# A hybrid encoder layer: the u tiles read from a transposed copy, the low parts of the v tiles on another engine

## The chip, the cores and the metric

The kernel runs on one core of one Trainium2 chip. The metric is the device time of one execution in microseconds, median of three runs. The engines are called as in the profile: PE (TensorE, with PEld for its weight loads), DVE (VectorE), ACT (ScalarE), POOL (GpSimd) and SP, which issues the plain transfers.

## What is computed

One layer of an encoder: projections, attention, two recurrent scans, and at its end a retrieval feed-forward over 16384 experts of one neuron each, which is the part that the change touches. For 1024 tokens of width 1024, eight heads choose 16 experts each, so 128 per token.

```python
def peer_ffn(h, w_query, sub_keys1, sub_keys2, expert_u, expert_v):
    ...
    v1, i1 = lax.top_k(s1, PEER_TOPK)
    v2, i2 = lax.top_k(s2, PEER_TOPK)
    cand = (v1[..., :, None] + v2[..., None, :]).reshape(T, PEER_HEADS, PEER_TOPK * PEER_TOPK)
    top_s, top_p = lax.top_k(cand, PEER_TOPK)
    ...
    def block(args):
        xc, ic, gc = args
        u = jnp.take(expert_u, ic, axis=0)
        act = jax.nn.gelu(jnp.einsum('cd,ced->ce', xc, u).astype(jnp.float32), approximate=False)
        vv = jnp.take(expert_v, ic, axis=0)
        return jnp.einsum('ce,ced->cd', (gc * act).astype(vv.dtype), vv)
```

## The kernel before

The first 1200 us are the rest of the layer. The retrieval then treats its eight blocks of 128 tokens in two ways.

**Three blocks gather.** For each of 128 choices, `fetch` (L1364) brings the rows of u that the 128 tokens want into a tile gu (128x1024), and later the rows of v into gv: one indirect transfer each, issued by POOL. DVE multiplies gu by the tokens and sums (L1392), and adds gv times its weight to gacc (L1400). `gathers` is called from all later stages to spread these 384 pairs; each fetch is tied to the latest POOL product by `pace`, so that it comes behind it in POOL's queue, and is written two choices ahead of its use (`LAG`). Four buffers each hold gu and gv in the last stage.

**Five blocks go dense.** All 16384 experts are computed for 640 tokens, in 128 tiles of 128 experts, with weights that are zero for experts that were not chosen. A tile n needs:

- `u_load` (L1439): the 128x1024 tile of u, one expert per partition, two buffers.
- `u_transpose`: PE transposes it in eight blocks of 128x128 into two put banks (L1449); from each bank ACT rounds the high part uTh (L1452), DVE subtracts to get the low part uTl (L1458).
- `act_half`, twice: 24 products of 128x320 in three terms (high by high, low by high, high by low, L317 to L319) into a bank pact, and the GELU on ACT (L1467). put and pact share a ring of three banks.
- `gate`: the activations times the dense weights, on POOL (L1794), split into ah on ACT (L1795) and al on DVE (L1796).
- `v_load` and `v_split`: half a v tile, 128x512, as vr (four buffers), vh on ACT (L1814), and vl = vr - vh on POOL (L1815). vh and vl have three buffers each.
- `v_steps`: five token blocks by three products (L1835 to L1837) into five banks py; after four tiles DVE adds the five banks into yac (L1844).

The first 65 tiles (`early`) are brought up to the GELU in the stages before and stored; the last stage reads them back (gl). 21 of them run beside the queries, 24 beside the choice of experts, 20 beside the making of the dense weights, where POOL, DVE and ACT make one-hot tiles `o` (L1720). In the last stage the tiles go in groups of four: while PE does the eight v steps of one group (two halves of four tiles), the gates of the next are made, and the two tiles of it that are not early go through u products, one after each half.

The order on each engine comes from the scheduler of the framework, from the order in which the calls are written and from the dependences; each engine then works through its queue in order. `split` forms are in float32 rounded for the PE (`FR`).

Of the kernel before, what the change touches and what calls it, by code (L numbers as in the profile page):

```python
# [8 lines left out]
F32 = mybir.dt.float32  # L9
FR = mybir.dt.float32r  # L10
# [3 lines left out]
AF = mybir.ActivationFunctionType  # L14
ALU = mybir.AluOpType
# [5 lines left out]
D = 1024  # L21
NB = 8
NK = 8
# [40 lines left out]
NGL = 2  # L64
NACC = 2
NWH = 2
ULP = (-1, 1)
NUR = 1
NS_ = 3
TC = 32  # L70
NSTB = 2
# [10 lines left out]
def body(tc, nc, I, out, dbg=None):  # L82
# [3 lines left out]
    with root:  # L86
# [21 lines left out]
        ident = ct([128, 128], "ident")  # L108
# [54 lines left out]
        def acp(o_, i_):  # L163
            nc.scalar.activation(o_, i_, AF.Copy)  # L164
# [56 lines left out]
        for k in range(NK):  # L221
            for i in range(2):
                a = slot("adw")
# [58 lines left out]
        def mod_steps():  # L282
# [22 lines left out]

            L = []
            for m in range(4):
                L += [lambda m=m, k=k: one(m, k) for k in range(NK)]
                L.append(lambda m=m: fin(m))
            return L  # L310

# [1018 lines left out]
        HT = TD // 2  # L1330
        NT = 128
        U, V = I["peer_u"][0], I["peer_v"][0]
        Ue = U.rearrange("(a b) d -> b a d", b=128)
        Ve = V.rearrange("(a b) d -> b a d", b=128)
        TW = "tile"
        pe = ES()
# [2 lines left out]
        lpa = pe.enter_context(tc.tile_pool(name="lpa", bufs=2, reuse_waits=TW))  # L1339
        pas = ES()  # L1340
        pa = [pas.enter_context(tc.tile_pool(name="pa", bufs=3, space=PSUM, reuse_waits=TW))]
# [80 lines left out]
        pace = [None]  # L1422
# [5 lines left out]
                next(gt, None)  # L1428


        uts, ats, urp = {}, {}, []
        early = [n for n in range(NT) if (n + 1) * NEARLY // NT > n * NEARLY // NT]
        seq = early + [n for n in range(NT) if n not in early]
        after = dict(zip(seq, seq[1:]))
        actd = dram.tile([NEARLY, 128, TD], F32, name="actd")

        def u_load(n):
            u = lpa.tile([128, D], F32, name="u", bufs=NU)
            nc.sync.dma_start(u, Ue[n])  # L1439
            uts[n] = [u]  # L1440

        def u_transpose(n, kh):
            if kh == 0:
                uts[n] += [lpa.tile([128, NK, 128], FR, name="uTh"), lpa.tile([128, NK, 128], FR, name="uTl")]
            u, uh, ul = uts[n]
            pt = pa[0].tile([128, 512], F32, name="put", tag="a")
            for i in range(4):
                k = kh * 4 + i
                nc.tensor.transpose(pt[:, i * 128:(i + 1) * 128], u[:, k * 128:(k + 1) * 128], ident)  # L1449
            ks = slice(kh * 4, kh * 4 + 4)  # L1450
            p3 = pt.rearrange("p (k e) -> p k e", k=4)
            nc.scalar.activation(uh[:, ks], p3, AF.Copy)  # L1452
            if n in early and early.index(n) <= ULP[0] and kh >= ULP[1]:
                ur = urp[0].tile([128, 512], F32, name="ur", bufs=NUR)
                acp(ur, pt)
                nc.gpsimd.tensor_tensor(ul[:, ks], ur.rearrange("p (k e) -> p k e", k=4), uh[:, ks], ALU.subtract)
            else:
                nc.vector.tensor_tensor(ul[:, ks], p3, uh[:, ks], ALU.subtract)  # L1458

        def act_half(n, hf):  # L1460
            _, uh, ul = uts[n]
            if hf == 0:
                ats[n] = lpa.tile([128, TD], F32, name="gl", bufs=NGL)
            sl = slice(hf * HT, hf * HT + HT)
            ps = pa[0].tile([128, 512], F32, name="pact", tag="a")
            mm3(ps[:, 0:HT], [(uh[:, k, :], ul[:, k, :], dTh[:, k, sl], dTl[:, k, sl]) for k in range(NK)])
            nc.scalar.activation(ats[n][:, sl], ps[:, 0:HT], AF.Gelu)  # L1467
            if hf == 1 and n in early:
                nc.sync.dma_start(actd[early.index(n)], ats[n])

        def tile_steps(n):
            L = [lambda: act_half(n, 0), lambda: act_half(n, 1)]
            if n in after:
                m = after[n]
                L = [lambda: u_transpose(m, 0), L[0], lambda: u_transpose(m, 1), L[1]]
                if m in after:
                    L[0] = lambda: (u_load(after[m]), u_transpose(m, 0))
            return L


        with ES() as qs:
            q1 = qs.enter_context(tc.tile_pool(name="q1", bufs=1, reuse_waits=TW))
            q2 = qs.enter_context(tc.tile_pool(name="q2", bufs=2, reuse_waits=TW))
            urp.append(q2)
            pq = qs.enter_context(tc.tile_pool(name="pq", bufs=5, space=PSUM, reuse_waits=TW))

            def qbank(name):
# [20 lines left out]
            pt = qbank("pt")  # L1508
# [156 lines left out]
            for L in hl[:NGB]:  # L1665
                for f in L:
                    f()
            u_transpose(seq[0], 0)
            u_transpose(seq[0], 1)
            merge((Q1, 0, 1), (sum(hl[NGB:], []), 0.1, HE))  # L1670
            cg, cd = [c_steps(tb) for tb in range(NGB)], [c_steps(tb) for tb in range(NGB, NB)]
            tl_ = [tile_steps(n) for n in early]
# [126 lines left out]
        vts = {}  # L1799
# [10 lines left out]
        def v_split(i):  # L1810
            if i < len(vseq) and not isinstance(vts[i], tuple):
                vh = lp.tile([128, 512], FR, name="vh", bufs=NV)
                vl = lp.tile([128, 512], FR, name="vl", bufs=NV)
                nc.scalar.activation(vh, vts[i], AF.Copy)  # L1814
                pace[0] = nc.gpsimd.tensor_tensor(vl, vts[i], vh, ALU.subtract)  # L1815
                vts[i] = vh, vl

        def v_steps(g):
# [49 lines left out]
        for g in range(NT // GR + 1):  # L1868
# [3 lines left out]
            if g < NT // GR:  # L1872
                at(s0, g_load, g)
                for k, n in enumerate(order[g]):
# [3 lines left out]
                    else:  # L1878
                        L = tile_steps(n)
                        if TRY and n in after:  # L1880
                            L = [L[1], lambda L=L, k=k: (L[3](), [at(now[0] + TRY[i], L[2 * i]) for i in range(2)])]
# [37 lines left out]
```

## Time and profile before

| | |
|---|---|
| three runs | 4042.25, 4057.20, 4059.28 us (median 4057.2) |
| the profiled execution | 4056.53 us, its span 4054.8 us |
| PE busy over the span | 3468.1 us (86%), granted clock 0.928 |
| DVE | 3047.6 us (75%) |
| POOL | 2316.8 us (57%) |
| ACT | 1261.6 us (31%) |
| transposes of u | 1024 on PE, 1215.6 to 3981.3 us |
| vl on POOL | 256, 2404.1 to 4038.4 us |

Busy time counts an engine's instructions; the products of PE are pipelined and overlap each other. The granted clock is a share of the full TensorE clock. A wait is put down to the engine that released it last. "issue" as a releaser is time for which the profile names no other engine.

### The profile page before, as it was taken

The page shows a single profiled execution, that of the slowest core. Times are in us where ns is not written, and L with a number is a line of the kernel's source. Part 1 is how long each engine was busy: PE and PEld are TensorE (multiplying, and loading weights), DVE is VectorE, ACT ScalarE, POOL GpSimd, SP SyncE. Part 2 cuts the span into 40 slices and gives each one's busy share as a digit, 9 for nine tenths or more (in the row PEclk, how much of TensorE's full clock was granted, in tenths as well). Part 3 has the DMA queues.
Part 4 walks back from the last instruction along what each step waited for, and adds up shares of the span by engine and source line. Part 5 has one row for each costly group of instructions (what it writes and reads, how often), then busy time and mean ns, then how long its engine had stood idle before and what let it go on. Part 6 is the DMA issues. An engine that isn't in the chain of part 4 may idle for free. (4 is left out here: it accounts for less than half of the span.)

```text
span 4054.8 us, 62013 instructions
## 1 busy us (share of the span) xinstructions
PE 3468.1 (86%) x22961; PEld 3038.1 (75%) x22961; DVE 3047.6 (75%) x6082; ACT 1261.6 (31%) x2528; POOL 2316.8 (57%) x1762
## 2 busy tenths in 40 slices
PE   5978899988787878988888878889888988889898
PEld 4757877776787877878877766777777877777787
DVE  6776556776567999799788877777677878877765
ACT  3244344444213222222555532221222222222221
POOL 2132112221434466366699978777777877878774
PEclk9978998888898989999999989999899999999999
DMA  6543444343445366466798998777788888777774
GB/s 191 178 144 103 141 116 98 97 111 104 136 164 184 104 219 238 141 218 214 239 296 278 301 309 277 264 259 269 255 273 285 281 272 275 272 265 271 256 258 154
DMA packets 493462, 862.81 MB, mean 213 GB/s; under 512 B 149348, under 2 KB 290404, under 8 KB 489064
## 3 DMA queue, kind: packets, MB, share of 16 engines
q1 hardware_dynamic: 372840, 447.20, 34.3%
q0 software_dynamic: 113280, 411.63, 29.7%
q8 instruction: 181, 2.97, 0.3%
q10 hardware_dynamic: 7040, 0.03, 0.1%
q14 instruction: 121, 0.99, 0.1%
HBM read 741.91 MB, written 116.80 MB: 212 GB/s over the span
## 5 line engine op out<-in xcount | busy, mean ns | idle before, releaser
L1392 DVE SCALAR_TENSOR_TENSOR gu<-gu,ghr 128x1024 f32<-128x1024 f32 x384 | 590.3, 1538 | 301.5 <-DMA gu<-in_peer_u_dram,ei 296.2
L317 PE MATMUL pact<-dTh,uTh 128*128 128x320 f32 x2048 | 663.6, 324 | 72.2 <-DVE uTl L1458 68.3
L1400 DVE SCALAR_TENSOR_TENSOR gacc<-gv,gact,gacc 128x1024 f32<-128x1024 f32 x381 | 614.0, 1611 | 117.1 <-DMA gv<-in_peer_v_dram,ei 116.1
L319 PE MATMUL pact<-dTh,uTl 128*128 128x320 f32 x2048 | 651.3, 318 | 19.2 <-DVE uTl L1458 19.2
L318 PE MATMUL pact<-dTl,uTh 128*128 128x320 f32 x2048 | 650.3, 318 | 0.0
L1835 PE MATMUL py<-vh,ah 128*128 128x512 f32 x1280 | 531.7, 419 | 137.5 <-DVE yac L1844 77.4
L1364 POOL DMA_INDIRECT gu<-in_peer_u_dram,ei x384 | 517.9, 1349 | 86.2 <-issue 44.2
L1836 PE MATMUL py<-vl,ah 128*128 128x512 f32 x1280 | 529.1, 413 | 38.2 <-POOL vl L1815 38.2
L1364 POOL DMA_INDIRECT gv<-in_peer_v_dram,ei x384 | 477.9, 1245 | 115.0 <-issue 101.5
L1837 PE MATMUL py<-vh,al 128*128 128x512 f32 x1280 | 523.7, 409 | 4.5 <-DVE al L1796 4.5
L317 PEld LDWEIGHTS pact<-dTh,uTh 128*128 128x128 f32 x2048 | 400.8, 196 | 89.4 <-DVE uTl L1458 78.5
L1815 POOL TENSOR_TENSOR vl<-vr,vh 128x512 fp32r<-128x512 f32 x256 | 367.2, 1435 | 146.1 <-issue 116.5
L1835 PEld LDWEIGHTS py<-vh,ah 128*128 128x128 f32 x1280 | 254.9, 199 | 218.0 <-ACT vh L1814 68.8
L319 PEld LDWEIGHTS pact<-dTh,uTl 128*128 128x128 f32 x2048 | 400.1, 195 | 21.4 <-DVE uTl L1458 21.3
L318 PEld LDWEIGHTS pact<-dTl,uTh 128*128 128x128 f32 x2048 | 400.6, 196 | 2.6
L1836 PEld LDWEIGHTS py<-vl,ah 128*128 128x128 f32 x1280 | 255.2, 199 | 99.6 <-POOL vl L1815 51.4
L1467 ACT ACTIVATE gl<-pact 128x320 f32<-128x320 f32 x256 | 111.2, 437 | 632.8 <-PE pact L319 601.1
L1837 PEld LDWEIGHTS py<-vh,al 128*128 128x128 f32 x1280 | 255.2, 199 | 62.0 <-DVE al L1796 6.8
L1795 ACT ACTIVATE ah<-gl 128x640 fp32r<-128x640 f32 x128 | 92.7, 737 | 653.6 <-POOL gl L1794 552.0
L1720 POOL TENSOR_SCALAR o<-io,tT 128x128 f32<-128x128 f32 x160 | 232.5, 1457 | 35.7 <-ACT tT L164 27.5
L1741 PE MATMUL pgb<-o,o 128*128 128x128 f32 x1280 | 184.0, 290 | 64.8 <-POOL o L1720 56.4
L1814 ACT ACTIVATE vh<-vr 128x512 fp32r<-128x512 f32 x256 | 157.0, 624 | 226.3 <-PE py L1837 181.8
(1445 smaller groups left out, 7527.1 us busy)
## 6 DMA issues: line engine op xcount, KB each, us to landing
u<-in_peer_u_dram SPq DMA_DIRECT2D x128, 512.0 KB, 5.8
vr<-in_peer_v_dram SPq DMA_DIRECT2D x256, 256.0 KB, 4.0
Gd<-st SPq DMA_DIRECT2D x160, 256.0 KB, 7.1
actd<-gl SPq DMA_DIRECT2D x65, 320.0 KB, 4.4
gl<-actd SPq DMA_DIRECT2D x65, 320.0 KB, 4.8
awt<-in_ada_w_dram SPq DMA_DIRECT2D x32, 512.0 KB, 6.4
wraw<-in_peer_w_query_dram SPq DMA_DIRECT2D x32, 512.0 KB, 4.0
wraw<-in_w_in_dram SPq DMA_DIRECT2D x26, 512.0 KB, 5.1
```

Of the source, the lines that this page charges most:

```text
L317: nc.tensor.matmul(ps, lh, rh, start=(i == 0), stop=False)
L318: nc.tensor.matmul(ps, lh, rl, start=False, stop=False)
L319: nc.tensor.matmul(ps, ll, rh, start=False, stop=(i == n - 1))
L1364: g_ = nc.gpsimd.indirect_dma_start(out=r_, out_offset=None, in_=src, in_offset=bass.IndirectOffsetOnAxis(ap=eid[tb][:, j:j + 1], axis=0))
L1392: nc.vector.scalar_tensor_tensor(u, u, 1.0, hr, op0=ALU.mult, op1=ALU.mult, accum_out=act[:, q:q + 1])
L1400: nc.vector.scalar_tensor_tensor(acc, v, pact[:, q:q + 1], acc, op0=ALU.mult, op1=ALU.add)
L1720: r_ = eng.tensor_scalar(o1[:, q], io128, tT[:, 0, t:t + 1], tT[:, 2, t:t + 1], op0=ALU.is_equal, op1=ALU.mult)
L1741: nc.tensor.matmul(pg[:, q * 128:(q + 1) * 128], o1[:, 4 * x_ + q], o2[:, 4 * x_ + q], start=True, stop=True)
L1815: pace[0] = nc.gpsimd.tensor_tensor(vl, vts[i], vh, ALU.subtract)
L1835: nc.tensor.matmul(ys[hf][b], ah[:, ts], vh, start=(n == tiles[0]), stop=False)
L1836: nc.tensor.matmul(ys[hf][b], ah[:, ts], vl, start=False, stop=False)
L1837: nc.tensor.matmul(ys[hf][b], al[:, ts], vh, start=False, stop=(n == tiles[-1]))
```

## The change

The host writes a second copy of u beside the first, in which tile n already lies with the model dimension on the partitions. `u_load` reads that copy, `u_split` replaces `u_transpose`: one ACT copy and one DVE subtraction of 128x1024, both from SBUF, and no work on PE. The gathers go on reading the first copy. In `v_split` the subtraction goes to DVE, and `pace` is then set by the gate alone. The step that was the second pair of transposes is left empty, so that the number of steps stays.

```diff
-        Ue = U.rearrange("(a b) d -> b a d", b=128)
+        Ut = I["peer_ut"]
...
         def u_load(n):
+            if n in uts:
+                return
             u = lpa.tile([128, D], F32, name="u", bufs=NU)
-            nc.sync.dma_start(u, Ue[n])
+            nc.sync.dma_start(u, Ut[n])
             uts[n] = [u]
...
-        def u_transpose(n, kh):
...
-            for i in range(4):
-                k = kh * 4 + i
-                nc.tensor.transpose(pt[:, i * 128:(i + 1) * 128], u[:, k * 128:(k + 1) * 128], ident)
...
-            nc.scalar.activation(uh[:, ks], p3, AF.Copy)
...
-                nc.vector.tensor_tensor(ul[:, ks], p3, uh[:, ks], ALU.subtract)
+        def u_split(n):
+            u_load(n)
+            if len(uts[n]) > 1:
+                return
+            u = uts[n][0]
+            uh, ul = lpa.tile([128, NK, 128], FR, name="uTh"), lpa.tile([128, NK, 128], FR, name="uTl")
+            u3 = u.rearrange("p (k e) -> p k e", k=NK)
+            nc.scalar.activation(uh, u3, AF.Copy)
+            nc.vector.tensor_tensor(ul, u3, uh, ALU.subtract)
+            uts[n] += [uh, ul]
...
-                L = [lambda: u_transpose(m, 0), L[0], lambda: u_transpose(m, 1), L[1]]
+                L = [lambda: u_split(m), L[0], lambda: None, L[1]]
...
-                pace[0] = nc.gpsimd.tensor_tensor(vl, vts[i], vh, ALU.subtract)
+                nc.vector.tensor_tensor(vl, vts[i], vh, ALU.subtract)
...
+    a = inputs["peer_u"]
+    a = _np.ascontiguousarray(_np.asarray(a)[0].reshape(128, 128, NK, 128).transpose(1, 3, 2, 0)).reshape(128, 128, D)
+    arrays["in_peer_ut_dram"] = a
```

POOL's queue in the last stage, before: gl is the gate product, vl the low part, gu and gv the gathers.

```order
L1794 TENSOR_TENSOR gl_34594<-gl_34594,gt__34536 128x640
L1815 TENSOR_TENSOR vl_34694<-vr_34538,vh_34693 128x512
L1364 DMA gu_34712<-in_peer_u_dram,ei2_11948 128x1024
L1364 DMA gv_34714<-in_peer_v_dram,ei2_11948 128x1024
L1815 TENSOR_TENSOR vl_34744<-vr_34567,vh_34743 128x512
L1364 DMA gu_34762<-in_peer_u_dram,ei2_11948 128x1024
L1364 DMA gv_34764<-in_peer_v_dram,ei2_11948 128x1024
```

The same queue now:

```order
L1786 TENSOR_TENSOR gl_32587<-gl_32587,gt__32300 128x640
L1362 DMA gu_32706<-in_peer_u_dram,ei2_11948 128x1024
L1362 DMA gv_32708<-in_peer_v_dram,ei2_11948 128x1024
L1362 DMA gu_32735<-in_peer_u_dram,ei2_11948 128x1024
L1362 DMA gv_32737<-in_peer_v_dram,ei2_11948 128x1024
L1362 DMA gu_32769<-in_peer_u_dram,ei2_11948 128x1024
L1362 DMA gv_32771<-in_peer_v_dram,ei2_11948 128x1024
```

Between two pairs of gathers there stood a vl; now up to four pairs follow each other, with only gl between.

DVE's queue in the last stage, before, from the last of the five additions on:

```order
L1844 TENSOR_TENSOR yac4_23250<-yac4_23250,py_33665 128x512
L1400 SCALAR_TENSOR_TENSOR gacc_29896<-gv_33897,gact_32957,gacc_29896 128x1024
L1392 SCALAR_TENSOR_TENSOR gu_33945,gact_33745<-gu_33945,ghr_29100 128x1024
L1400 SCALAR_TENSOR_TENSOR gacc_29896<-gv_33947,gact_32957,gacc_29896 128x1024
L1392 SCALAR_TENSOR_TENSOR gu_33977,gact_33745<-gu_33977,ghr_29100 128x1024
L1400 SCALAR_TENSOR_TENSOR gacc_29896<-gv_33979,gact_32957,gacc_29896 128x1024
L1796 TENSOR_TENSOR al_33952<-gl_33816,ah_33951 128x640
L1458 TENSOR_TENSOR uTl_33909<-put_33910,uTh_33908 128x512
L1458 TENSOR_TENSOR uTl_33909<-put_33917,uTh_33908 128x512
```

And now, from behind the last of the five additions:

```order
L1807 TENSOR_TENSOR vl_32110<-vr_31945,vh_32109 128x512
L1390 SCALAR_TENSOR_TENSOR gu_32000,gact_31589<-gu_32000,ghr_27960 128x1024
L1788 TENSOR_TENSOR al_32097<-gl_31972,ah_32096 128x640
L1398 SCALAR_TENSOR_TENSOR gacc_28708<-gv_32002,gact_30854,gacc_28708 128x1024
L1807 TENSOR_TENSOR vl_32142<-vr_31974,vh_32141 128x512
L1390 SCALAR_TENSOR_TENSOR gu_32090,gact_31589<-gu_32090,ghr_27960 128x1024
L1398 SCALAR_TENSOR_TENSOR gacc_28708<-gv_32092,gact_30854,gacc_28708 128x1024
L1390 SCALAR_TENSOR_TENSOR gu_32128,gact_31589<-gu_32128,ghr_27960 128x1024
L1398 SCALAR_TENSOR_TENSOR gacc_28708<-gv_32130,gact_30854,gacc_28708 128x1024
L1450 TENSOR_TENSOR uTl_32292<-u_32101,uTh_32291 128x1024
L1788 TENSOR_TENSOR al_32135<-gl_32011,ah_32134 128x640
L1807 TENSOR_TENSOR vl_32169<-vr_32069,vh_32168 128x512
```

The low parts of v stand between the gathered operations, with one or two pairs of them between two vl, and uTl is one operation from u and uTh.

## Rows read from the trace of the kernel before

**Rows 1.** First line of the page.

```profile
span 4054.8 us, 62013 instructions
```

**Rows 2.** Busy time by stretch: length, PE, PEld, DVE, ACT, POOL, clock, DMA, GB/s.

```profile
1360.00:1680.00 320.00, 269.26 (x1762) 264.29 (x1760) 291.04 (x998) 85.30 (x162) 163.40 (x108) 0.91 0.53 180
1680.00:1925.00 245.00, 203.65 (x1316) 196.62 (x1316) 243.54 (x612) 56.27 (x104) 154.76 (x103) 0.94 0.64 217
1925.00:2370.00 445.00, 373.97 (x2599) 353.12 (x2598) 363.28 (x654) 250.34 (x594) 380.92 (x278) 0.95 0.86 279
2390.00:4055.00 1665.00, 1462.95 (x7280) 1246.11 (x7279) 1243.00 (x1361) 353.81 (x656) 1266.63 (x894) 0.95 0.77 263
```

**Rows 3.** Groups, 2390 to 4055: busy us, mean ns | idle before, releasers.

```profile
L1835 PE MATMUL py<-vh,ah 128*128 128x512 f32 x1280 | 531.7, 419 | 137.5 <-DVE yac L1844 77.4 <-ACT vh L1814 59.6
L1836 PE MATMUL py<-vl,ah 128*128 128x512 f32 x1280 | 529.1, 413 | 38.2 <-POOL vl L1815 38.2
...
L1400 DVE SCALAR_TENSOR_TENSOR gacc<-gv,gact,gacc 128x1024 f32<-128x1024 f32 x262 | 437.6, 1670 | 99.9 <-DMA gv<-in_peer_v_dram,ei 99.1
L1392 DVE SCALAR_TENSOR_TENSOR gu<-gu,ghr 128x1024 f32<-128x1024 f32 x248 | 409.8, 1653 | 273.3 <-DMA gu<-in_peer_u_dram,ei 273.1
L1815 POOL TENSOR_TENSOR vl<-vr,vh 128x512 fp32r<-128x512 f32 x256 | 367.2, 1435 | 146.1 <-issue 116.5 <-ACT vh L1814 24.7 <-DVE yac L1844 2.1
L1364 POOL DMA_INDIRECT gu<-in_peer_u_dram,ei x247 | 338.3, 1370 | 40.3 <-issue 27.3 <-ACT vh L1814 1.1 <-DVE uTl L1458 0.8
L1364 POOL DMA_INDIRECT gv<-in_peer_v_dram,ei x264 | 334.5, 1267 | 78.0 <-issue 72.0 <-DVE gu L1392 3.7 <-DVE yac L1844 1.7
...
L1844 DVE TENSOR_TENSOR yac<-yac,py 128x512 f32<-128x512 f32 x310 | 195.3, 677 | 17.0 <-PE py L1837 17.0
...
L1796 DVE TENSOR_TENSOR al<-gl,ah 128x640 fp32r<-128x640 f32 x127 | 129.1, 1033 | 25.0 <-ACT ah L1795 24.9
...
L1458 DVE TENSOR_TENSOR uTl<-put,uTh 128x512 fp32r<-128x512 f32 x122 | 78.1, 678 | 0.9 <-ACT uTh L1452 0.5
```

**Rows 4.** Waits, 2390 to 4020: us in total, times, longest us.

```profile
ACT ah L1795 <- POOL gl L1794: 542.7, 92, 14.2
```

**Rows 5.** Timeline, 3105 to 3116: start us, us, engine, line [idle before].

```profile
3105.83 0.61 ACT L1814 ACTIVATE vh<-vr 128x512 fp32r<-128x512 f32 x1
...
3106.58 1.53 POOL L1815 TENSOR_TENSOR vl<-vr,vh 128x512 fp32r<-128x512 f32 x1 [1.42 <-issue]
3108.26 1.39 POOL L1364 DMA_INDIRECT gu<-in_peer_u_dram,ei  x1
...
3115.69 2.83 DVE L1392 SCALAR_TENSOR_TENSOR gu<-gu,ghr 128x1024 f32<-128x1024 f32 x1 [4.51 <-DMA gu<-in_peer_u_dram,ei]
```

**Rows 6.** Timeline of PE, 2545 to 2547: eight transposes and the next product.

```profile
2545.36 1.04 PE L1449 MATMUL put<-ident,u 128*128 128x128 f32 x8
2546.15 0.48 PE L1835 MATMUL py<-vh,ah 128*128 128x512 f32 x1
```

**Rows 7.** Single lines, whole span: duration ns min/median/max, first and last start.

```profile
L1392 DVE SCALAR_TENSOR_TENSOR gu<-gu,ghr x384: 1195/1221/7777, 1403.3 to 3909.9; 128x1024 f32<-128x1024 f32 x192
L1400 DVE SCALAR_TENSOR_TENSOR gacc<-gv,gact,gacc x381: 1220/1284/4451, 1472.5 to 3997.2; 128x1024 f32<-128x1024 f32 x191
L1796 DVE TENSOR_TENSOR al<-gl,ah x128: 807/815/2648, 2389.1 to 4020.4; 128x640 fp32r<-128x640 f32 x128
L1415 DVE TENSOR_TENSOR gacc<-gacc,gr x3: 1209/1216/2551, 2444.4 to 4000.8; 128x1024 f32<-128x1024 f32 x3
L1857 DVE TENSOR_TENSOR yac<-yac,gr x10: 684/688/691, 4029.7 to 4050.0; 128x512 f32<-128x512 f32 x10
```

**Rows 8.** Busy time of L1794 (gl on POOL) in the last stage.

```profile
2390.00:4055.00 1665.00, 228.54 (x127) 0.95 0.77 263
```

**Rows 9.** Groups, of 1680 to 1925 and of 1925 to 2370.

```profile
L1400 DVE SCALAR_TENSOR_TENSOR gacc<-gv,gact,gacc 128x1024 f32<-128x1024 f32 x31 | 56.0, 1806 | 0.0
...
L1720 POOL TENSOR_SCALAR o<-io,tT 128x128 f32<-128x128 f32 x160 | 232.5, 1457 | 35.7 <-ACT tT L164 27.5 <-issue 6.2
```

More of the change, by code (lines that the diff above doesn't have):

```diff
@@ L66 @@
 NWH = 2
-ULP = (-1, 1)
-NUR = 1
 NS_ = 3
@@ L1428, in gathers @@
                 next(gt, None)
-        uts, ats, urp = {}, {}, []
+        uts, ats = {}, {}
         early = [n for n in range(NT) if (n + 1) * NEARLY // NT > n * NEARLY // NT]
@@ L1437, in u_load @@
         def u_load(n):
+            if n in uts:
+                return
             u = lpa.tile([128, D], F32, name="u", bufs=NU)
-            nc.sync.dma_start(u, Ue[n])
+            nc.sync.dma_start(u, Ut[n])
             uts[n] = [u]
-        def u_transpose(n, kh):
[L1443 to L1446, printed above, removed]
-            for i in range(4):
-                k = kh * 4 + i
-                nc.tensor.transpose(pt[:, i * 128:(i + 1) * 128], u[:, k * 128:(k + 1) * 128], ident)
-            ks = slice(kh * 4, kh * 4 + 4)
-            p3 = pt.rearrange("p (k e) -> p k e", k=4)
-            nc.scalar.activation(uh[:, ks], p3, AF.Copy)
[L1453 to L1457, printed above, removed]
-                nc.vector.tensor_tensor(ul[:, ks], p3, uh[:, ks], ALU.subtract)
+        def u_split(n):
[8 more added lines that the diff above has]
+            uts[n] += [uh, ul]
         def act_half(n, hf):
+            u_split(n)
             _, uh, ul = uts[n]
@@ L1474, in tile_steps @@
                 m = after[n]
-                L = [lambda: u_transpose(m, 0), L[0], lambda: u_transpose(m, 1), L[1]]
+                L = [lambda: u_split(m), L[0], lambda: None, L[1]]
                 if m in after:
-                    L[0] = lambda: (u_load(after[m]), u_transpose(m, 0))
+                    L[0] = lambda: (u_load(after[m]), u_split(m))
             return L
@@ L1483, in body @@
             q2 = qs.enter_context(tc.tile_pool(name="q2", bufs=2, reuse_waits=TW))
-            urp.append(q2)
             pq = qs.enter_context(tc.tile_pool(name="pq", bufs=5, space=PSUM, reuse_waits=TW))
@@ L1667, in body @@
                     f()
-            u_transpose(seq[0], 0)
-            u_transpose(seq[0], 1)
+            u_split(seq[0])
             merge((Q1, 0, 1), (sum(hl[NGB:], []), 0.1, HE))
@@ L1913 @@
         args[name] = nc.dram_tensor(f"in_{name}_dram", a.shape, mybir.dt.from_np(a.dtype), kind="ExternalInput").ap()
+    a = inputs["peer_u"]
+    a = _np.ascontiguousarray(_np.asarray(a)[0].reshape(128, 128, NK, 128).transpose(1, 3, 2, 0)).reshape(128, 128, D)
+    arrays["in_peer_ut_dram"] = a
+    args["peer_ut"] = nc.dram_tensor("in_peer_ut_dram", a.shape, mybir.dt.from_np(a.dtype), kind="ExternalInput").ap()
     o = nc.dram_tensor("out_0_dram", (1, T, D), F32, kind="ExternalOutput").ap()
```

## Prediction

> **What bounds the kernel now.** I read first the table by stage, then the groups of the last stage with the idle time before them, then the waits, then two short pieces of the timeline. The span is 4054.8 us [rows 1]; the profiled execution took 4056.53 us, so 1.7 us lie around the span, and it stands 0.7 us under the median of 4057.2 us. I make the sum against 4056.5.
>
> Four stretches contain nearly everything that the change touches [rows 2]. From 1360 to 1680 us queries and 21 early u tiles share the core; DVE is busy 291 of 320 us, PE 269. From 1680 to 1925 DVE is busy 243.5 of 245 us: it is the bound. From 1925 to 2370 POOL is busiest, 381 of 445 us. The dense stage from 2390 to the end, 1665 us, is where both edits meet: PE is busy 1463 us at a granted clock of 0.95, DVE 1243, POOL 1267, the DMA engines 77%. No engine is full there; the stage is three in-order queues waiting for each other.
>
> The waits say how. PE is idle 202 us (1665 - 1463): 77.4 for the additions that empty the py banks (DVE) and 59.6 for vh (ACT), both ahead of L1835, and 38.2 for vl (POOL) ahead of L1836 [rows 3]. ACT itself sits 542.7 us behind ah, waiting for the gate product on POOL [rows 4], and vh is queued behind ah. DVE is idle 422 us, of which 372 are waits for gathered rows: 273 ahead of gu, 99 ahead of gacc [rows 3]. A piece of timeline shows why they come late: POOL waits 1.42 us for a vl to start, which it does 0.14 us after ACT has ended its vh (3105.83 + 0.61), works on it 1.53 us, only then issues a gather at 3108.26, and DVE stands 4.51 us until a gather has landed, at 3115.69 [rows 5]. POOL is thus the engine that feeds DVE, and the 256 vl (367.2 us of work and 146.1 us of waiting before them, [rows 3]) sit in the middle of its queue.
>
> **The change part by part.** *Transposes out.* A tile had 8 transposes. Eight in a row start at 2545.36 and the next product starts at 2546.15 [rows 6]: 0.79 us of PE per tile. The dense stage has 122 halves uTl, so 61 tiles [rows 3]: 61 x 0.79 = 48 us less PE work, 1463 - 48 = 1415. In the three stretches before, 21 + 24 + 20 = 65 tiles give 51 us at most, but there PE waits for others.
>
> *u split from SBUF.* Two DVE operations of 0.678 us per tile become one of 128x1024. The nearest row is a plain SBUF operation of that size, 1.21 us at the least [rows 7], so 61 x 1.21 = 74 against 78.1 us [rows 3]: no gain to speak of. ACT's copy changes in the same way, and ACT is busy 354 of 1665 us [rows 2], which hides it.
>
> *vl from POOL to DVE.* POOL loses 367 of its 1267 us. DVE gets 256 operations of 128x512; the row with two SBUF inputs of that shape is 0.688 us [rows 7], so +176 us. DVE's sum becomes 1243 - 78 + 74 + 176 = 1415 us, the same as PE's. But DVE operations with two SBUF inputs are now stretched when POOL works beside them: gacc has mean 1.670 against a median of 1.284, gu 1.653 against 1.221, al 1.033 against 0.815 [rows 3, 7], together 262 x 0.386 + 248 x 0.432 + 127 x 0.218 = 236 us, while yac, which has one input in PSUM, keeps 0.677 [rows 3]. POOL's products in the stage are vl 367 and gl 228.5 us [rows 3, 8]; vl is 62% of them, so 146 us of the stretch should go with it. DVE then lies between 1415 (no relief) and 1269 us (relief by share); I take the middle, about 1340.
>
> The rule behind the stretch is in the Trainium skill, SBUF — State Buffer, section Who interferes with whom: a VectorE instruction with two SBUF inputs and a GpSimd instruction that reads SBUF exclude each other for the whole instruction. It speaks against the first edit: uTl had one input in PSUM and will have two in SBUF, as vl has on its new engine. If each of the 61 uTl waited for a whole gl of 1.80 us [rows 8], that would be 110 us more on DVE; by the shares above it is some 25.
>
> *Where the waits go.* On POOL the gathers no longer stand behind vl, which waits for vh, which waits for a vh buffer that PE must free. They stand behind gl and behind the release of one of four row buffers of each kind, which DVE gives back. So gathers should be issued further ahead and the 372 us shrink. The new wait: vl is now in DVE's queue behind gathered operations, with PE behind it. The order on DVE has one or two gather pairs between two vl; a pair is 1.28 + 1.22 = 2.5 us [rows 7], so up to 5 us for a step of PE that takes 15 products. Three vh buffers let DVE run ahead by two steps. For PE I leave the vl wait at its present 38 us, with DVE for POOL; I take away half of the vh wait (30 us), since ACT gets gl earlier, and some 40% of the py wait (32 us), since DVE idles less before the additions. With the transposes: -48 - 30 - 32 = -110 us for the dense stage. The ends are -48 - 202 (every PE wait gone) and, above nothing, the third rival below.
>
> *Earlier stages.* From 1680 DVE decides: 24 tiles, each 2 x 0.678 - 1.21 = 0.15 us less, against a stretch such as gacc shows there (1.806 against 1.284, [rows 9]), 0.52 us, if uTl gets it too: +9 us at most. From 1925 POOL decides, with 160 one-hot operations of 1.457 us [rows 9]; 20 tiles of transposes off PE do nothing for it, and if each uTl held POOL for its whole 1.21 us it would be +24 us. From 1360, 21 x 0.79 = 17 us less PE work, where PE is idle 51 of 320 us. Between -51 and +33 I take -12 us, since only the first of the three has PE near its end.
>
> Sum: 4056.5 - 110 - 12 = 3934.5, so **3934 us**, 3.0% less.
>
> **The rivals.** *First, the queues come apart more than that.* If the gathers are far enough ahead that DVE hardly waits, PE is left with its 1415 us and some 60 us of waits: 1475 for the dense stage, -190, and -25 before it: about 3840 us. For it: DVE at 1269 to 1340 us leaves room, and the DMA engines, 0.77 x 1665 = 1282 us, too. Against: three sums within 10% of each other rarely run without waits, and in each half DVE must add five banks before PE can go on.
>
> *Second, DVE takes the place of POOL and little is won.* No relief, since the remaining 127 gl find DVE with two SBUF inputs nearly always: 1415 us, half the gather waits (186) and the other 50 of its idle time: 1651 us, -14, and nothing before it: about 4040 us. The rule cited above is this one's reason. For it: DVE's sum has grown to that of PE. Against: gl alone would have to cause the stretch that vl and gl cause now.
>
> *Third, slower.* DVE serves its queue in order, so a vl behind a gather that has not landed stops PE. If the gather waits stay at 372 us although POOL is free, because landing and not issue sets them, DVE needs 1269 + 372 + 50 = 1691 us, +26: about 4083 us; without relief 1837, +172: 4228 us. It decides from the point where the remaining gather waits exceed 346 us (with relief) or 200 us (without). For it: a wait as long as 4.51 us [rows 5] is more than the vl buffers cover in one step. Against: the same gathers' wait began with POOL's late issue.
>
> That the change does not do what it says can be left out: in the new order PE has no transpose of u, and POOL no vl.
>
> **How the numbers follow.** Forecast 0.50 (own range 3885 to 3990), first rival 0.20 (3800 to 3885), second 0.18 (3990 to 4077), third 0.12. The range leaves out the outer part of the first rival and most of the third: 3835 to 4060. A difference under 0.5%, 20 us, can hardly be told from none here, since the runs before lie 17 us apart. Faster by more: 0.50 + 0.20 + 0.10 of the second = 0.80; within: the other 0.08; slower: 0.12.
>
> **What would show it.** Right, step by step: POOL's busy time in the dense stage falls by about 367 us; waits of gu and gacc for their DMA fall below 200 us; gacc and gu have means near 1.4 us; vl on DVE takes 0.69 us; PE waits less for yac and vh, and its wait for vl names DVE. The stretch from 1680 to 2370 keeps its length. Wrong: gu waits as long as before with POOL idle (third rival), gacc still at 1.65 us (second), or PE idle over 202 us with DVE vl as its releaser.

## The result and the profile after

The changed kernel takes **3919.6 us** (median, 3914.6 to 3922.8) against 4057.9 us of the kernel before on the same chip: a ratio of 0.9667 with a 95% interval of 0.9645 to 0.9690. The forecast was 3934 us. The profiled execution took 3917.25 us, its span is 3915.5 us, 139 us less than before. In the text a stage begins with its first product: the dense stage with the first py, the weights stretch before it with the first pgb. The busy times of after by these marks (length, PE, PEld, DVE, ACT, POOL, granted clock, DMA, GB/s):

```profile
1303.60:1923.70 620.10, 518.77 (x3298) 507.99 (x3297) 601.01 (x1888) 161.66 (x286) 354.44 (x224) 0.92 0.59 196
1923.70:2370.40 446.70, 340.52 (x2255) 320.90 (x2254) 354.63 (x607) 238.25 (x549) 398.76 (x279) 0.90 0.87 280
2370.40:3915.50 1545.10, 1387.90 (x6792) 1190.03 (x6792) 1204.51 (x1556) 353.90 (x594) 844.96 (x638) 0.95 0.77 283
```

By the same marks the three stretches of before are 646.4, 434.8 and 1665.2 us long. The dense stage gives 120 us, the queries and the choice of experts 26, the 1304 us ahead of them 5 (less than the 17 us by which single executions of the kernel before differ), and the weights stretch takes 12 back. In the dense stage [rows 2] POOL's busy time falls from 1267 to 845 us, DVE's from 1243 to 1205, PE's from 1463 to 1388. PE's idle time falls from 202 to 157 us.

The groups of the dense stage of after, 2370 to the end, answer to [rows 3] (busy us, mean ns | idle before, releasers):

```profile
L1828 PE MATMUL py<-vl,ah 128*128 128x512 f32 x1280 | 527.6, 412 | 64.1 <-DVE vl L1807 63.5
L1827 PE MATMUL py<-vh,ah 128*128 128x512 f32 x1280 | 523.7, 410 | 93.1 <-DVE yac L1836 64.3 <-ACT vh L1806 13.9 <-ACT uTh L1449 9.3
...
L1398 DVE SCALAR_TENSOR_TENSOR gacc<-gv,gact,gacc 128x1024 f32<-128x1024 f32 x262 | 360.0, 1374 | 55.5 <-DMA gv<-in_peer_v_dram,ei 50.6 <-issue 4.6
L1390 DVE SCALAR_TENSOR_TENSOR gu<-gu,ghr 128x1024 f32<-128x1024 f32 x248 | 320.2, 1292 | 138.2 <-DMA gu<-in_peer_u_dram,ei 131.8 <-issue 6.4
...
L1836 DVE TENSOR_TENSOR yac<-yac,py 128x512 f32<-128x512 f32 x310 | 190.5, 675 | 0.9 <-PE py L1829 0.8
...
L1807 DVE TENSOR_TENSOR vl<-vr,vh 128x512 fp32r<-128x512 f32 x256 | 181.5, 713 | 12.6 <-ACT vh L1806 12.6
L1788 DVE TENSOR_TENSOR al<-gl,ah 128x640 fp32r<-128x640 f32 x128 | 103.7, 830 | 130.3 <-ACT ah L1787 130.3
L1450 DVE TENSOR_TENSOR uTl<-u,uTh 128x1024 fp32r<-128x1024 f32 x60 | 83.5, 1392 | 5.9 <-ACT uTh L1449 5.9
```

DVE's waits for gathered rows have gone from 372 to 182 us (131.8 + 50.6). The stretch of its operations with two SBUF inputs is mostly gone: gacc from 1.670 to 1.374 us, gu from 1.653 to 1.292, al from 1.033 to 0.830, while yac keeps its 0.675. PE waits less for yac and vh, and more for vl, which is DVE's now. The waits behind the gate answer to [rows 4] (us in total, times, longest):

```profile
ACT ah L1787 <- POOL gl L1786: 287.9, 62, 7.8
POOL gl L1786 <- DMA gl<-actd: 252.6, 22, 17.8
DVE al L1788 <- ACT ah L1787: 130.3, 32, 10.9
```

ACT's wait for the gate product has halved. Another stands behind it: POOL waits 253 us, up to 17.8 us at a time, for the early tiles' activations to be loaded into a gl buffer. A piece of the timeline shows what hangs on one such wait (start us, us, engine, line [idle before]):

```profile
3017.74 1.56 POOL L1786 TENSOR_TENSOR gl<-gl,gt__27670 128x640 f32<-128x640 f32 x1 [16.15 <-DMA gl<-actd]
3019.26 1.57 POOL L1786 TENSOR_TENSOR gl<-gl,gt__27290 128x640 f32<-128x640 f32 x1
3020.98 0.98 POOL L1362 DMA_INDIRECT gu<-in_peer_u_dram,ei  x1
...
3029.88 0.94 POOL L1362 DMA_INDIRECT gv<-in_peer_v_dram,ei  x1 [0.30 <-issue]
...
3020.86 1.37 ACT L1787 ACTIVATE ah<-gl 128x640 fp32r<-128x640 f32 x2 [4.65 <-POOL gl L1786]
...
3021.64 1.56 DVE L1788 TENSOR_TENSOR al<-gl,ah 128x640 fp32r<-128x640 f32 x2 [4.30 <-ACT ah L1787]
...
3028.64 1.26 DVE L1390 SCALAR_TENSOR_TENSOR gu<-gu,ghr 128x1024 f32<-128x1024 f32 x1 [4.84 <-DMA gu<-in_peer_u_dram,ei]
```

POOL stands for 16 us. ACT and DVE then stand over 4 us each for the gate, eight gathers leave in one burst from 3020.98 on, and DVE stands once more until the first has landed. SP, which issues the load, shows why it came late (start us, us, engine, line):

```profile
3004.41 9.21 SPq L1800 DMA_DIRECT2D vr<-in_peer_v_dram  x3
3013.71 0.38 SPq L1776 DMA_DIRECT2D gl<-actd  x1
```

The load of gl leaves right behind three loads of vr that took up SP's queue for 9.21 us. Over the stage (2400 to 3900 us) SP waits for these buffers:

```profile
SPq L1800 <- DVE vl L1807: 837.3, 229, 11.1
...
SPq L1776 <- DVE al L1788: 48.1, 31, 8.4
```

A vr buffer comes free when DVE has made vl from it, a gl buffer when DVE has made al. SP thus waits 837 us for the former and 48 us for the latter.

### The profile page after: what moved, and what is told of

Read it like the earlier page. It is cut to its first block, busy times and chain, and to the rows that moved or that the text cites. A ratio compares the mean times of both kernels' runs of the same rounds, so it can differ in the third digit from the quotient of the medians.

```text
span 3915.5 us, 59807 instructions
## 1 busy us (share of the span) xinstructions
PE 3337.0 (85%) x21937; PEld 2929.5 (75%) x21937; DVE 3016.5 (77%) x6210; ACT 1248.9 (32%) x2400; POOL 1929.2 (49%) x1506
## 5 line engine op out<-in xcount | busy, mean ns | idle before, releaser
L315 PE MATMUL pact<-dTh,uTh 128*128 128x320 f32 x2048 | 652.6, 319 | 10.1 <-ACT gl L1461 6.1
L1390 DVE SCALAR_TENSOR_TENSOR gu<-gu,ghr 128x1024 f32<-128x1024 f32 x384 | 505.0, 1316 | 162.8 <-DMA gu<-in_peer_u_dram,ei 150.4
L1827 PE MATMUL py<-vh,ah 128*128 128x512 f32 x1280 | 523.7, 410 | 93.1 <-DVE yac L1836 64.3
L1398 DVE SCALAR_TENSOR_TENSOR gacc<-gv,gact,gacc 128x1024 f32<-128x1024 f32 x381 | 533.3, 1400 | 72.4 <-DMA gv<-in_peer_v_dram,ei 67.5
L1362 POOL DMA_INDIRECT gu<-in_peer_u_dram,ei x384 | 504.0, 1313 | 123.6 <-issue 65.8
L1362 POOL DMA_INDIRECT gv<-in_peer_v_dram,ei x384 | 457.4, 1191 | 131.4 <-issue 103.0
L1733 PE MATMUL pgb<-o,o 128*128 128x128 f32 x1280 | 194.7, 300 | 80.7 <-POOL o L1712 76.8
L1712 POOL TENSOR_SCALAR o<-io,tT 128x128 f32<-128x128 f32 x160 | 244.5, 1533 | 11.7 <-ACT tT L162 9.3
L1733 PEld LDWEIGHTS pgb<-o,o 128*128 128x128 f32 x1280 | 174.3, 208 | 97.3 <-POOL o L1712 92.3
L1788 DVE TENSOR_TENSOR al<-gl,ah 128x640 fp32r<-128x640 f32 x128 | 103.7, 830 | 130.3 <-ACT ah L1787 130.3
```

The costliest lines, as they stand in the source:

```text
L315: nc.tensor.matmul(ps, lh, rh, start=(i == 0), stop=False)
L1362: g_ = nc.gpsimd.indirect_dma_start(out=r_, out_offset=None, in_=src, in_offset=bass.IndirectOffsetOnAxis(ap=eid[tb][:, j:j + 1], axis=0))
L1390: nc.vector.scalar_tensor_tensor(u, u, 1.0, hr, op0=ALU.mult, op1=ALU.mult, accum_out=act[:, q:q + 1])
L1398: nc.vector.scalar_tensor_tensor(acc, v, pact[:, q:q + 1], acc, op0=ALU.mult, op1=ALU.add)
L1712: r_ = eng.tensor_scalar(o1[:, q], io128, tT[:, 0, t:t + 1], tT[:, 2, t:t + 1], op0=ALU.is_equal, op1=ALU.mult)
L1733: nc.tensor.matmul(pg[:, q * 128:(q + 1) * 128], o1[:, 4 * x_ + q], o2[:, 4 * x_ + q], start=True, stop=True)
```

## The experiments

Ratios are to the kernel before, run beside the experiments on the same chip. Four chips were used, and its median on them was 4044.6, 4047.6, 4051.0 and 4051.4 us, so that ratios, not times, are compared between chips. Lengths of stages and waits are those of one profiled execution of each kernel; the executions of one kernel lie 3 to 28 us apart, those of the kernel before up to 45.

**1. Each edit alone.** The first is after with vl back on POOL:

```
-                nc.vector.tensor_tensor(vl, vts[i], vh, ALU.subtract)
+                pace[0] = nc.gpsimd.tensor_tensor(vl, vts[i], vh, ALU.subtract)
```

> Only the u tiles are changed (transposed copy, split from SBUF); vl stays on GpSimd and sets the pace. Theory (the gain comes from freeing GpSimd's queue): the matrix engine loses 48 us of transposes in the dense stage, but DVE's waits for gathers stay near 372 us and the stretch of gacc near 1.67 us; the time is 20 to 50 us under before, 4005 to 4040 us. Rival (the transposes were the cost): most of the 138 us are here, 3910 to 3960 us.

3998.1 us, ratio 0.9890 (0.9850 to 0.9929). Its dense stage is 1628 us, 37 less than before, and the stages ahead are 18 us shorter. Groups of its dense stage:

```profile
L1398 DVE SCALAR_TENSOR_TENSOR gacc<-gv,gact,gacc 128x1024 f32<-128x1024 f32 x262 | 430.8, 1644 | 93.1 <-DMA gv<-in_peer_v_dram,ei 90.9
L1390 DVE SCALAR_TENSOR_TENSOR gu<-gu,ghr 128x1024 f32<-128x1024 f32 x248 | 427.6, 1725 | 211.8 <-DMA gu<-in_peer_u_dram,ei 198.6 <-issue 12.2 <-DMA ghr<-h2d 0.4
...
L1450 DVE TENSOR_TENSOR uTl<-u,uTh 128x1024 fp32r<-128x1024 f32 x60 | 105.6, 1759 | 0.0
```

The stretch stays as in before, and the new uTl, read from SBUF, gets it too: its mean is 1.759 us here and 1.392 in after. DVE's waits for gathered rows were expected to stay near 372 us; they are 290 us (198.6 + 90.9), with every vl still in POOL's queue.

The second is before with vl on DVE, the reverse of the same two lines.

> Only vl moves to DVE; the transposes stay on the matrix engine. Theory: waits of gu and gacc for their DMA fall from 372 us below 220 us and gacc's mean from 1.67 to about 1.4 us; 70 to 110 us under before, 3945 to 3990 us. Rival (the transposes were the cost): at most 30 us under before, 4025 us or more.

3939.6 us, ratio 0.9744 (0.9707 to 0.9781). Its dense stage is 1552 us, 113 less. Its stretch and its products:

```profile
2390.00:3942.80 1552.80, 1419.49 (x7280) 1236.59 (x7280) 1210.74 (x1618) 354.99 (x658) 824.12 (x639) 0.96 0.77 283
```
```profile
L1835 PE MATMUL py<-vh,ah 128*128 128x512 f32 x1280 | 525.8, 411 | 96.1 <-DVE yac L1844 92.1 <-ACT vh L1814 2.9 <-ACT ah L1795 1.1
L1836 PE MATMUL py<-vl,ah 128*128 128x512 f32 x1280 | 518.6, 405 | 20.4 <-DVE vl L1815 20.4
```

DVE's waits for gathered rows are 142 us. The v edit alone brings three quarters of the gain. Alone the edits give 37 and 113 us in the dense stage, together 120: with vl gone from POOL, the transposes that leave PE are worth only 7 us there, which the scatter of single executions can hide. PE's busy time fell from 1463 to 1419 us with all 7280 products in place, since the same products take 411 and 405 ns instead of 419 and 413.

**2. Is it POOL's queue, or POOL's reads of SBUF?** Three kernels put work back on POOL beside after's vl on DVE; the gathers are tied to it as they were to vl, and its results go to the tile cc, which held constants of earlier stages and which the dense stage doesn't read. First, memsets, which read nothing:

```
                 nc.vector.tensor_tensor(vl, vts[i], vh, ALU.subtract)
+                for _ in range(5):
+                    pace[0] = nc.gpsimd.memset(cc, 0.0)
```

> The changed kernel, with five extra fills of 128x256 on GpSimd for every v tile, at the place in its queue where vl stood; they take about as long as a vl (5 x 0.25 to 0.3 us), read no SBUF, wait for nothing, and their result is not used. Theory, if the mere length of GpSimd's queue makes the gathers late: 40 to 90 us over the changed kernel, 3960 to 4010 us, gather waits on DVE back over 300 us, gacc still at about 1.37 us. Rival, if what mattered is that vl read SBUF beside DVE, or that it waited for vh: within 15 us of the changed kernel, 3905 to 3935 us.

4053.3 us, ratio 1.0025 (1.0000 to 1.0050): all of the gain is gone, more than the 40 to 90 us that were expected.

```profile
L1398 DVE SCALAR_TENSOR_TENSOR gacc<-gv,gact,gacc 128x1024 f32<-128x1024 f32 x262 | 362.1, 1382 | 119.0 <-DMA gv<-in_peer_v_dram,ei 117.5 <-DVE gu L1390 0.5
L1809 POOL MEMSET cc<- 128x256 f32 x1143 | 361.0, 316 | 51.3
```
```profile
ACT ah L1787 <- POOL gl L1786: 724.6, 96, 17.8
```

POOL is busy 1219 us again, ACT waits 725 us for the gate, DVE 280 us for gathers, and gacc stays at 1.382 us. The memsets wait for nothing, so 137 of the 1280 run ahead of the dense stage, the first at 2266 us: the weights stretch, where POOL is the busiest engine, grows to 475 us from after's 447. The dense stage itself is 1655 us, 110 more than after's and 10 less than before's, with 361 us of memsets in the place of 367 us of vl. Second, the subtraction itself in two halves:

```
+                for o_ in (0, 256):
+                    pace[0] = nc.gpsimd.tensor_tensor(cc, vts[i][:, o_:o_ + 256], vh[:, o_:o_ + 256], ALU.subtract)
```

> The changed kernel, and GpSimd does each subtraction of vh from vr as well, in two halves into a scratch tile that nobody reads: its queue, its reads of SBUF and its wait for vh are as before the change, but no product waits for it. Theory: the three together give back most of the gain of the v edit, 80 to 120 us over the changed kernel, 4000 to 4040 us, with gacc at 1.6 us or more. If only the length of the queue mattered, this is equal to the run with fills; if only the reads did, this one is slow and that one is not.

4160.3 us, ratio 1.0274 (1.0227 to 1.0322), some 240 us over the changed kernel and not 80 to 120. The work put back came out larger than vl's: 512 halves of 1.056 us are 540 us, not 367.

```profile
L1830 PE MATMUL py<-vl,ah 128*128 128x512 f32 x1280 | 558.9, 437 | 225.3 <-DVE vl L1807 225.2
...
L1809 POOL TENSOR_TENSOR cc<-vr,vh 128x256 f32<-128x256 f32 x512 | 540.4, 1056 | 146.4 <-issue 116.3 <-ACT vh L1806 7.8
L1398 DVE SCALAR_TENSOR_TENSOR gacc<-gv,gact,gacc 128x1024 f32<-128x1024 f32 x262 | 404.3, 1543 | 116.7 <-DMA gv<-in_peer_v_dram,ei 108.8 <-issue 6.4
```

Third, therefore, one half and one memset, which keep POOL busy in the dense stage for as long as the memsets did:

```
+                nc.gpsimd.memset(cc, 0.0)
+                pace[0] = nc.gpsimd.tensor_tensor(cc, vts[i][:, 0:256], vh[:, 0:256], ALU.subtract)
```

> As the run with fills, but of the extra work on GpSimd per v tile one piece is a subtraction of 128x256 from vr and vh (1.06 us in the run that did two of them) and one a fill (0.32 us): 1.38 us together, where the fills took 1.58 us. Equal length in GpSimd's queue, but it reads SBUF and waits for vh. Theory (the length of the queue is the cost, the stretch of DVE comes on top): gacc near 1.5 us, 10 to 70 us over the run with fills. Rival (the fills' cost is all there is): within 10 us of the run with fills, with gacc at 1.38 us.

4002.9 us, ratio 0.9902 (0.9871 to 0.9934): faster than the memsets alone, against the expectation.

```profile
L1398 DVE SCALAR_TENSOR_TENSOR gacc<-gv,gact,gacc 128x1024 f32<-128x1024 f32 x262 | 386.3, 1475 | 97.4 <-DMA gv<-in_peer_v_dram,ei 96.0
L1809 POOL TENSOR_TENSOR cc<-vr,vh 128x256 f32<-128x256 f32 x256 | 265.8, 1038 | 149.8 <-issue 126.1 <-ACT vh L1806 7.8 <-POOL cc L1808 2.2
...
L1450 DVE TENSOR_TENSOR uTl<-u,uTh 128x1024 fp32r<-128x1024 f32 x60 | 100.1, 1668 | 0.0
```

POOL is busy 1220 us in both. The reads stretch gacc to 1.475 us and lift DVE from 1243 to 1324 us busy, and yet the time is 50 us less. Between the two profiled executions some 30 us of this lie in the weights stretch (475 against 445 us), into which only the memsets ran ahead, and 32 in the dense stage (1655 against 1623). Both kernels give back most of the gain, so time on POOL is a cost of its own; it is not the whole of it, since the same 1220 us go with two lengths of the dense stage, and why is not settled. The stretch of DVE by itself does not show in the time: the kernel that has it is the faster.

**3. The loads of gl.** After's new wait has three explanations: the place of the load in the order, the SP queue in which it stands behind other loads, or its buffers, two that loaded and computed activations share. First, `gate_load` written three steps ahead of its gate instead of two:

```
-GD = 2
+GD = 3
```

> The changed kernel with the loads of stored activations (gl) written three steps ahead of their use, not two. Theory: GpSimd's wait for gl, 253 us in the dense stage, comes from their place behind v loads in SyncE's queue; one step earlier takes away a third or more of it, and the time falls by 10 to 40 us, 3870 to 3905 us. Rival (the two gl buffers hold the load back, not its place): within 10 us of the changed kernel.

3919.5 us, ratio 0.9693 (0.9660 to 0.9726), POOL's wait 238 us: no change, where 10 to 40 us were expected. Then the loads issued from ACT's queue:

```
-                nc.sync.dma_start(ats[n], actd[early.index(n)])
+                nc.scalar.dma_start(ats[n], actd[early.index(n)])
```

> The changed kernel with the same loads issued by ScalarE, so that no v load stands before them. Theory: GpSimd's wait for gl falls below 120 us and DVE's waits for gathers below 150 us; 3860 to 3900 us. Rival: ScalarE now waits for a free gl buffer with vh queued behind it; the matrix engine's wait for vh grows past 40 us and the time is that of the changed kernel or up to 40 us more.

3891.5 us, ratio 0.9616 (0.9584 to 0.9647). The wait is 183 us and DVE's for gathers 187; below 120 and below 150 were expected. Standing behind the v loads in SP's queue costs 28 us against the run above. Then two buffers of its own for the loaded gl, paid for with one of the six buffers each of ah and al:

```
-NU, NAH, NV = 2, 6, 3
+NU, NAH, NV = 2, 5, 3
...
-                ats[n] = lpa.tile([128, TD], F32, name="gl", bufs=NGL)
+                ats[n] = lp.tile([128, TD], F32, name="gle", bufs=2)
```

> The changed kernel with two buffers of their own for the loaded gl, beside the two for computed ones; for the room, ah and al have five buffers, not six. Theory of the queue: little, within 15 us of the changed kernel, since the loads still stand behind v loads. Rival (buffers hold the loads back): GpSimd's wait for gl halves and the time falls by 20 to 60 us.

3853.9 us, ratio 0.9534 (0.9503 to 0.9565). The time falls by 66 us against the first of these kernels, a little more than the 20 to 60 expected of the buffers; the dense stage is 1471 us, 74 less than after's. Its waits, and its two first products:

```profile
POOL gl L1786 <- ACT gl L1461: 193.7, 45, 23.0
POOL gle L1786 <- DMA gle<-actd: 179.3, 42, 13.7
...
ACT ah L1787 <- POOL gl L1786: 72.2, 32, 3.2
```
```profile
L1828 PE MATMUL py<-vl,ah 128*128 128x512 f32 x1280 | 522.3, 408 | 105.3 <-DVE vl L1807 105.2
...
L1827 PE MATMUL py<-vh,ah 128*128 128x512 f32 x1280 | 509.8, 401 | 12.2 <-ACT vh L1806 7.6 <-DVE yac L1836 4.7
```

ACT's wait falls from 288 to 72 us, and PE's for vh and yac from 78 to 12. POOL still waits 179 us for loads, so that wait did not halve, and now 194 us for the GELU on ACT (42 in after); little of either reaches PE. DVE's waits for gathers stay as they were (119 + 62 against 132 + 51). So it was the gate, not the gathers, that held PE for these 74 us in after. Did it in before? The same two lines in the kernel before:

> The kernel before, with the two own buffers for loaded gl (ah and al five, not six), vl on GpSimd and the transposes in place. Theory (the gl buffers bind only once GpSimd is free of vl): within 20 us of before. Rival (they bound all along, and the v edit only found another way round): 50 us or more under before.

3931.0 us, ratio 0.9699 (0.9665 to 0.9733): the buffers alone are worth about what the whole change is, as the rival had it.

```profile
L1400 DVE SCALAR_TENSOR_TENSOR gacc<-gv,gact,gacc 128x1024 f32<-128x1024 f32 x262 | 514.6, 1964 | 77.8 <-DMA gv<-in_peer_v_dram,ei 75.2 <-issue 1.6 <-DVE gu L1392 0.4
L1392 DVE SCALAR_TENSOR_TENSOR gu<-gu,ghr 128x1024 f32<-128x1024 f32 x248 | 396.5, 1599 | 112.9 <-DMA gu<-in_peer_u_dram,ei 103.7 <-issue 5.8 <-DMA ghr<-h2d 2.9
```
```profile
ACT ah L1795 <- POOL gl L1794: 176.2, 37, 9.4
```

POOL is as full as in before, 1267 us, and gacc is stretched to 1.964 us, more than in before. Still ACT's wait falls from 543 to 176 us and DVE's for gathers from 372 to 179, and the dense stage loses 125 us.

How the buffers do it is not shown. In the kernel before, POOL stood only this long for loads of gl (2390 to 4020 us):

```profile
POOL gl L1794 <- DMA gl<-actd: 57.9, 29, 5.0
```

That is less than half of the 125 us. SP's own waits for a buffer of these loads did not fall with the two extra buffers either: 106 us in the kernel before and 234 here, 48 in after and 55 there with the buffers. The edit is shown to give the time; that a load stood and waited for a buffer is not. No run tells apart whether the number of buffers counts or that the loads have their own.

**4. What is left, and the transposes again.** In the kernel with its own gl buffers PE waits 105 us for vl. Its splits of v (vh and vl) were written one step ahead:

```
-VAH = 0
+VAH = 1
```

> Both edits and the gl buffers, and each v tile is split one step ahead of its use. Theory: of the 105 us that the matrix engine still waits for vl behind DVE's gathers, a third or more goes; 15 to 50 us under the run without it. Rival (the scheduler already placed vl as early as its three buffers let it): within 10 us of it.

3854.2 us, ratio 0.9508 (0.9474 to 0.9542); PE's wait for vl is 104.8 us. No change. Then the v edit and the gl buffers without the u edit, transposes and all:

> The kernel with only the v edit, and the same gl buffers; the transposes of u stay. Against the run that has both edits and these buffers it prices the transposes where the other waits are smallest. Theory (then the matrix engine's 48 us of transposes in the dense stage lie on the path in full): 45 to 75 us over that run, with the 18 us of the earlier stages in it. Rival (DVE or the gathers decide there): under 30 us.

3843.2 us, ratio 0.9479 (0.9443 to 0.9514), where 45 to 75 us over the kernels with the u edit and the buffers were expected. It is 11 us under the one with the splits a step ahead, on the same chip, and under the other by its ratio (0.9479 against 0.9534). Its weights stretch and dense stage, and a group of the latter:

```profile
1951.20:2391.30 440.10, 359.53 (x2508) 338.20 (x2507) 352.92 (x627) 244.08 (x579) 385.99 (x280) 0.96 0.89 288
2391.30:3845.10 1453.80, 1382.65 (x7237) 1210.26 (x7237) 1216.47 (x1616) 358.62 (x650) 841.15 (x636) 0.98 0.81 301
```
```profile
L1836 PE MATMUL py<-vl,ah 128*128 128x512 f32 x1280 | 508.4, 397 | 36.8 <-DVE vl L1815 36.3
```

PE is busy 33 us longer than without the transposes (1382.7 against 1349.9), at a mean granted clock of 0.98 against 0.96, and idle 50 us less; the wait for vl alone is 69 us shorter, 36 against 105. So the u edit loses 17 us in the dense stage (both kernels with the u edit and the buffers have 1471 us there, both without it for the late tiles 1454 and 1450) and gains its 20 or so before it. Then each tile its better way: the copy for the 65 early tiles, the transposes for the late ones.

```
-            nc.sync.dma_start(u, Ue[n])
+            nc.sync.dma_start(u, I["peer_ut"][n] if n in early else Ue[n])
```

> The low parts of v on VectorE and the two buffers for the loaded selections, as in the run before that kept all transposes (3843 us, 0.948 of the kernel before); now the 65 early u tiles alone come from the transposed copy, the late ones are still transposed on TensorE. My theory: the 17 to 19 us that the u edit took from the stages before the dense one are its own and stay, and the dense stage keeps its length of about 1454 us: 3815 to 3835 us, ratio 0.941 to 0.947. Rival: what the early stages gain is lost again at the start of the dense stage, or VectorE's higher share there takes it: 3838 to 3850 us, ratio 0.947 to 0.951.

**3827.3 us**, ratio 0.9441 (0.9422 to 0.9459), as expected, the fastest of all and 92 us under the changed kernel (0.944 against 0.967). The runs, 3823 to 3831 us, lie under all of those of the run before it (3837 to 3849), which was on another chip with the same median of the kernel before.

```profile
1923.50:2376.10 452.60, 354.23 (x2313) 333.27 (x2312) 355.83 (x611) 239.98 (x556) 402.14 (x281) 0.90 0.86 277
2376.10:3826.30 1450.20, 1379.37 (x7237) 1207.52 (x7237) 1219.57 (x1616) 358.36 (x650) 827.15 (x636) 0.98 0.81 302
```

The dense stage keeps its length (1450 against 1454 us). The weights stretch begins 28 us earlier and is 12.5 us longer, the same 12 that after lost there. Its groups there, first without the u edit (1951 to 2391), then with it (1923.5 to 2376):

```profile
L1720 POOL TENSOR_SCALAR o<-io,tT 128x128 f32<-128x128 f32 x158 | 229.2, 1454 | 9.5 <-issue 7.5
L1741 PE MATMUL pgb<-o,o 128*128 128x128 f32 x1280 | 185.1, 291 | 72.0 <-POOL o L1720 63.7 <-DVE o L1720 7.8
```
```profile
L1726 POOL TENSOR_SCALAR o<-io,tT 128x128 f32<-128x128 f32 x159 | 241.3, 1521 | 5.1 <-issue 3.1
L1747 PE MATMUL pgb<-o,o 128*128 128x128 f32 x1280 | 199.8, 306 | 82.6 <-POOL o L1726 78.7 <-DVE o L1726 3.2
```

POOL's one-hot operations take 0.067 us more each beside a uTl that reads SBUF twice. PE waits 15 us more for them, and its products there take 306 instead of 291 ns, at a mean granted clock of 0.90 instead of 0.96.

## Why the prediction was right, and where its steps were not

The time lies 14 us under the forecast, the dense stage at -120 against -110, the stages before at -19 against -12. The steps behind the sum fared less evenly, and that it came out so near is in part luck.

| step | predicted | measured |
|---|---|---|
| POOL's busy time in the dense stage | -367 us | -422 |
| gather waits of DVE | 372 to under 200 | 182 |
| DVE's busy time | 1340, from 1269 to 1415 | 1205 |
| vl on DVE | 0.69 us each | 0.713 |
| PE's busy time | -48 | -75 |
| PE's wait for yac | -32 | -13 |
| PE's wait for vh | -30 | -46 |
| PE's wait for vl | 0 | +25, DVE its releaser |
| earlier stages | -12 | -19 |

**The first step held**: vl in POOL's in-order queue cost the time, and taking it out gave the time. The v edit alone takes 113 us off the dense stage, and still 86 (1540 to 1454) where the gl buffers are added. The memsets, which put the same length back on POOL, without a read and with vl on DVE, take 110 of the 120 us away again.

**But the path from there was only in part the one predicted.** The prediction put the gain on the gathers behind vl and gave the gate 30 us, half of the vh wait. The runs with their own gl buffers put the gate first: there ACT's wait for gl falls and the time with it, in after with no change of the gather waits. The gather waits fell below 200 us as predicted, but they fall to 179 us in the kernel before with the buffers alone, with all vl on POOL, and to 290 with the u edit alone. So their fall does not show that it was vl that stood before them. The 542.7 us of [rows 4] named POOL, which was busy with vl, gathers and the gate's own wait; that freeing POOL would leave it waiting 253 us for a load was in no step of the sum. Two buffers for the loaded gl give another 66 us: 3919.5 us with the load one step earlier, which changed nothing, and 3853.9 us with the buffers, on the same chip. Time on POOL and the gl buffers were two limits side by side: with the transposes in place the dense stage is 1665 us with neither edit, 1552 with vl off POOL, 1540 with the buffers and 1454 with both.

**PE's work** fell by 75 us and not 48. The same products took 1 to 9 ns less each, which makes some 16 us; the sum had no term for that. The rest, some 59 us, is more than the spacing of the transposes gave. With the waits, which fell by 45 and not 62 us, the stage came out near the forecast: two errors of opposite sign.

**The stretch on DVE** was relieved by more than the share of POOL's products that left: gu, gacc and al lost 90 + 78 + 25 = 193 of the 236 us, not 146, let alone the middle of the range. It had little to say in the time: the run with memsets and the one with reads part the two, and DVE was not the bound in either. On the rule of the Trainium skill, SBUF — State Buffer, section Who interferes with whom: the trace agrees that a POOL operation that reads SBUF stretches DVE's operations with two SBUF inputs (gacc 1.475 to 1.964 us where POOL subtracts, 1.362 to 1.405 where it doesn't, memsets or none) and leaves those with a PSUM input alone (yac 0.674 to 0.678 us in every run). Its 110 us for uTl did not come: the shortest uTl of after takes 1.194 us, and against it the mean of 1.392 us makes 60 x 0.20 = 12 us in after, and the 1.759 us with vl on POOL make 34 us.

**The transposes** were priced at 48 us on PE's path. Taking them out is worth 37 us in the dense stage with vl on POOL, 7 with vl on DVE, and -17 with the gl buffers added as well: what PE saves it waits for, once others are late. That PE's wait for vl is 69 us longer without transposes is measured; why was not tried.

**The earlier stages** gave 26 us in the queries and the choice of experts and lost 12 in the weights stretch, where the prediction saw a bound of +24 and then counted nothing. Of the 26 us, 22 lie ahead of the fourth block's first oe product on POOL (1671.8 us before, 1645.0 after), where the prediction looked for them, and 4 behind it. From this mark to the first py it is 718 us before and 725 after: the stretch from 1680 us nearly kept its length, with a gain and a loss inside it. In the queries and the choice PE's waits for uTl and for put's release sank from 87 us (65.6 + 11.2 + 10.3) to 50, but those for wl and qT grew from 7 to 48, and PE's idle time went from 95 to 101 us. What fell is its busy time, from 551 to 519 us.

**The rivals.** The first, 3840 us, did not come: DVE still waits 182 us for gathers and 130 behind the gate, and PE keeps 157 us of waits, not some 60. The extra buffers bring about its time (3854 us). The second had the gather waits right (186 us) and fell with the stretch, most of which went. The third fell with the gather waits, which are not above 346 us.

## What to carry to other kernels

When an in-order queue is relieved, ask what its next instruction waits for: here the gate on POOL waited for a load, and two more buffers for the loads gave 66 us. They gave 120 us in the kernel before as well, where the wait was booked as waiting for POOL. Follow a long wait for an engine through that engine's own queue, and through the buffers that its inputs need, before you move work. And price work taken off an engine anew after each other edit: the same transposes were worth 37, 7 and -17 us of the dense stage.

## What was not expected of the hardware

- Where transposes left PE, its mean granted clock was in places lower. In the weights stretch it was 0.94 to 0.96 in the four kernels with the transposes (PE busy 357 to 360 us of 434 to 440) and 0.87 to 0.92 in the ten with the copy (338 to 356 of 445 to 475). With the gl buffers and vl on DVE the dense stage had 0.98 with transposes and 0.96 without, but from before to after it kept 0.95. These are means between the two levels of 1.2 and 2.4 GHz; the py products took 395 to 400 ns where the mean was 0.98 and 401 to 408 where it was 0.96. Whether the transposes or the longer waits set the clock, no run tells apart.
- The subtraction that POOL does in 1.435 us takes DVE 0.713 (128x512). Half of it (128x256) still takes POOL 1.038 to 1.056 us beside a busy DVE.
- POOL's one-hot operations went from 1.454 to 1.521 us when DVE's uTl began to read both inputs from SBUF. Over all kernels they take 1.436 to 1.458 us with the transposes and 1.479 to 1.526 with the copy. That the disturbance works both ways fits this; no run changes the read alone.
